# Down projection: ten steps of the second product ahead of the first product's last step

## The chip, the cores and the metric

The kernel runs on one core of one Trainium2 chip. The metric is device microseconds (us) of one execution. Engines are named as in the profile: PE is TensorE's matmul queue, PEld its weight loads, DVE is VectorE, ACT ScalarE, POOL GpSimd, SP SyncE. All DMAs of this kernel are issued from SP's queue, which the profile calls SPq.

## The reference, cut to what matters

A decoder trunk with two layers. Each layer ends with a gated feed-forward network. Its last product, `w_down`, is what the change touches; it runs once in each layer.

```python
D_MODEL, SEQ, DEPTH, D_FF = 1024, 1024, 2, 2816

def conv_ffn(h, w_up, conv_w, conv_b, w_down):
    u = h @ w_up
    ...
    a, b = u[..., :D_FF], u[..., D_FF:]
    return (jax.nn.silu(a) * b) @ w_down

for l in range(DEPTH):
    ...
    x = x + conv_ffn(rms_norm(x, ffn_norm[l]), w_up[l], conv_w[l], conv_b[l], w_down[l])
```

So the hidden activations are 1024 tokens by 2816 channels, and the down projection multiplies them by a 2816 x 1024 matrix.

## The kernel before

**Precision.** Each f32 operand is split into a high and a low part (`split`, L78): ACT writes the high part (L81), DVE subtracts it and writes the low part (L82). `mm3` (L153) issues three matmuls for each pair of tiles (L157 high by high, L158 high by low, L159 low by high).

**Seven products in place of eight.** `Up` (the up projection) and `Down` both use a Strassen-like scheme: the operands are cut into 2 x 2 blocks, and sums of blocks are multiplied seven times. For `Down` the left factors are the hidden activations. A hidden tile holds 128 channels by 1024 tokens, and there are 22. `Up.left` (L1355) takes tiles 2k and 2k+1 when both are done and makes seven factors of 128 x 512: four of them are halves of the tiles (one of these changed in place), and three are sums in buffers named `gs`. The sums are four POOL instructions (L1360 to L1363). `Up.store` (L1366) writes the seven factors to DRAM tile `gd_k`, with k from 0 to 10: two DMAs from the tiles (`gd<-v`), one from `gs`, two from the tiles, two from `gs`. The factors of the first and the second product are the first two written.

**Steps of Down.** A product i is a sum over k, so it has 11 steps (i, j), with j the index of the `gd` tile. In `Down.steps` (L1429) they stand product by product: (0, 0) to (0, 10), (1, 0) to (1, 10), and so on; `PRODUCTS` (L1419) says which factor and which block of `w_down` a product reads and where its sum goes. This text numbers steps by their place in the list: step 10 is the first product's last before the change. One step is 12 matmuls of 128 x 512: four row blocks times three. The first product sums into four PSUM banks named `psb` (`self.chain`), the second into four banks of two `psa` tiles. `add` (L1504) adds finished banks to x on DVE: after the second product both its own banks and the chain's; `psa` has two buffers, so the third product's first matmul waits for that add.

**Feeding a step.** `fetch` (L1448) reads the factors of two consecutive steps from `gd` into a `wr` tile (three buffers, L1457). `prep` (L1460) splits the factor and the block of `w_down` into `wh` and `wl` (four buffers each), three steps ahead of the step that is run, and calls `fetch` for pairs further on. The blocks of `w_down` are kept in SBUF (`hx` and `hT` tiles, `claim`, L1439), and `sums` (L1475) changes them in place on DVE for later products (L1478, L1480, L1482).

**What sets the order.** `Up.run` (L1372) is a table of slots: step 0 of Down is issued in slot 160, step 6 in slot 166, the last one; `left` and `store` of the last pair of hidden tiles stand in slots 164 and 166. After that `down_all` (L1116) issues the remaining steps. DVE's and ACT's order while `Up.run` is written is the order of the code; otherwise the framework's scheduler orders the instructions. SP's queue is in order: a DMA that waits for its data holds back every DMA behind it.

Of the kernel before, what the change touches and what calls it, by code (L numbers as in the profile page):

```python
# [22 lines left out]
CH = 512  # L23
# [19 lines left out]
class Trunk:  # L43
    def __init__(self, ctx, tc, a, out):
        self.tc, self.nc, self.a, self.out = tc, tc.nc, a, out
        e = ctx.enter_context
        self.cp = e(tc.tile_pool(name="cp", bufs=1))
        self.wp = e(tc.tile_pool(name="wp", bufs=1))
        self.hp = e(tc.tile_pool(name="hp", bufs=1))
        self.pp = e(tc.tile_pool(name="pp", bufs=1, space=PSUM))  # L50
        self.dp = e(tc.tile_pool(name="dp", bufs=1, space=DRAM))
        self.uid = 0
# [152 lines left out]
    def load_block(self, w, cols, gcol=None, step=2, pool=None):  # L205
        tiles = [self.load_rows(w, k0, min(step, KT - k0), cols, gcol, pool) for k0 in range(0, KT, step)]

        def at(kt, c0, n):
            hi, lo = tiles[kt // step]
            return hi[:, kt % step, c0:c0 + n], lo[:, kt % step, c0:c0 + n]  # L210
        return at
# [984 lines left out]
class Up:  # L1196
# [116 lines left out]
    def product(self, n, i):  # L1313

        s, add = self.st[n], self.k.nc.vector.tensor_tensor
        if i == 0:
            self.first(n)
        elif i == 1:
            self.second(n)
            self.take_second(n)  # L1320
        elif i == 2:
            self.third(n)
        elif i == 3:
            self.prod(n, s["c"], "s1", "t1", True)
            s["c5"] = self.copied(s["c"])
        elif i == 4:
            self.prod(n, s["p"], "s3", "t3", False)
            s["ub"] = self.k.sb(self.late, [P, S], F32, "u", 3)
            add(s["ub"][:, CH:], s["p"], s["c5"], ALU.add)
        elif i == 5:  # L1330
            self.prod(n, s["c"], "s4", "b22", False)
            add(s["ua"][:, CH:], s["c"], s["c2"], ALU.add)  # L1332
        else:
            self.prod(n, s["p"], "a22", "t4", False)
            self.k.nc.scalar.activation(s["ub"][:, :CH], s["p"], AF.Copy)
# [19 lines left out]
    def left(self, k):  # L1355

        g, h = self.hidden[2 * k:2 * k + 2]
        s1, s2, s4 = (self.k.sb(self.late, [P, CH], F32, "gs", 3) for _ in range(3))
        add = self.k.nc.gpsimd.tensor_tensor
        add(s1, g[:, CH:], h[:, CH:], ALU.add)  # L1360
        add(s2, s1, g[:, :CH], ALU.subtract)
        add(g[:, CH:], g[:, :CH], g[:, CH:], ALU.subtract)
        add(s4, h[:, :CH], s2, ALU.subtract)  # L1363
        self.factors = (g[:, :CH], h[:, :CH], s2, g[:, CH:], h[:, CH:], s1, s4)
# [49 lines left out]
class Down:  # L1414

    NK = NF // 2
# [5 lines left out]
    def __init__(self, k, l, gds, fx):  # L1422
        self.k, self.l, self.gds, self.fx = k, l, gds, fx
        self.w = k.a["w_down"][l]
        NK = self.NK
        self.names = {"x": [("b11", i) for i in range(NK)] + [("t3", i) for i in range(NK)] + [("b22", NK - 1)],
                      "h": [("b21", i) for i in range(NK)] + [(n, i) for i in range(NK) for n in ("b12", "b22")][:-1]}
        self.place = {}
        self.steps = [(i, j) for i in range(7) for j in range(NK)]  # L1429
        self.pairs = [(i, j, min(2, NK - j)) for i in range(7) for j in range(0, NK, 2)]  # L1430
        self.ready, self.raws, self.at_step = [], [], 0

    def claim_x(self):
# [26 lines left out]
    def prep(self, upto):  # L1460

        k = self.k
        while len(self.ready) < min(upto, len(self.steps)):
            i, j = self.steps[len(self.ready)]
            n = self.PRODUCTS[i][1]
            pair = i * (self.NK + 1) // 2 + j // 2
            self.fetch(pair + 1)
            hi, lo = k.whl([P, 2, CH])
            for x, src in enumerate((self.raws[pair][:, j % 2, :], self.place[n, j])):
                k.split(src, hi[:, x, :], lo[:, x, :])  # L1470
            self.ready.append((hi, lo))
            if j % 2 or j == self.NK - 1:
                self.fetch(pair + 4)
# [12 lines left out]
    def step(self):  # L1486
        k, n = self.k, self.at_step
        i, j = self.steps[n]
        _, _, run, dst = self.PRODUCTS[i]
        self.prep(n + 1 + self.AHEAD)  # L1490
        if n == 0:
            self.chain = [k.psb() for _ in range(4)]
        if j == 0:
            self.banks = self.chain if run else [t[:, x * CH:(x + 1) * CH] for t in (k.psa(), k.psa()) for x in range(2)]
        hi, lo = self.ready[n]
        first = i == 0 or not run
        for p in range(4):
            ps = slice(p * P, (p + 1) * P)
            k.mm3(self.banks[p], (hi[:, 0, ps], lo[:, 0, ps]), (hi[:, 1, :], lo[:, 1, :]), first and j == 0, j == self.NK - 1, not first)
        self.sums(i, j)  # L1500
        self.at_step += 1
        return i, j

    def add(self, i):  # L1504

        for banks in ((), (self.banks, self.chain))[i] if i < 2 else (self.banks,):
            for p in range(4):
                for rows, col in self.PRODUCTS[i][3]:
                    xs = self.k.x[:, rows * 4 + p, col * CH:(col + 1) * CH]
                    self.k.nc.vector.tensor_tensor(xs, banks[p], xs, ALU.add)  # L1510
# [57 lines left out]
```

## Time and profile before

| | |
|---|---|
| runs | 2602.53, 2613.72, 2611.74 us |
| median of the runs | 2611.74 us |
| profiled execution | span 2602.7 us; the profile gives no other time for it |
| PE busy | 2466.1 us (95%), 12306 matmuls |
| DVE busy | 1887.8 us (73%) |
| ACT busy | 1342.2 us (52%) |
| POOL busy | 751.8 us (29%) |
| chain that ended last | PE 71%, DVE 10%, ACT 6%, DMA 5%, POOL 4%, issue 3% |
| mean granted clock of PE | 0.988 of full speed |

The time line gives an instruction's start and length; "[10.22 <-ACT wh L81]" behind it means that its engine had stood idle for 10.22 us and what ended that. Buffer numbers are left out of names. Layer 0's down projection begins near 1156 us of the span, layer 1's near 2345 us.

### The profile page before, as it was taken

How to read it: one execution, taken by the hardware profiler on the slowest of the kernel's cores; microseconds unless marked ns; L12 is line 12 of the kernel's file. 1: busy time of each engine (PE TensorE's matmuls, PEld its weight loads, DVE VectorE, ACT ScalarE, POOL GpSimd, SP SyncE). 2: the span in 40 equal slices, each digit the busy share in tenths (PEclk: the TensorE clock that was granted, in tenths of full speed). 3: DMA queues.
4: the chain of work that ended last, by engine and by line, in shares of the span. 5: the costliest groups of instructions: out<-in, count | busy, mean ns of one | idle time of the engine just before them, and what ended most of it. 6: DMA issues, size and time to landing. Idle time of an engine off the chain costs nothing.

```text
span 2602.7 us, 35727 instructions
## 1 busy us (share of the span) xinstructions
PE 2466.1 (95%) x12306; PEld 2058.2 (79%) x12306; DVE 1887.8 (73%) x3207; ACT 1342.2 (52%) x2553; POOL 751.8 (29%) x616
## 2 busy tenths in 40 slices
PE   7898988988999999998999999999999999998998
PEld 7787777766778888886888988887777888886886
DVE  5757787888377878877665467878476778787765
ACT  5437777877145454443454356767244444443443
POOL 0105344444134554543000000000233455444000
PEclk9999999999999999999999999999999999999999
DMA  8473224333422333347334466666622233237523
GB/s 250 145 206 111 62 82 114 104 105 125 163 74 89 113 101 98 105 169 268 108 128 137 153 186 189 199 180 176 211 101 76 95 105 114 98 100 278 172 97 114
DMA packets 302701, 357.69 MB, mean 137 GB/s; under 512 B 37960, under 2 KB 183224, under 8 KB 302520
## 3 DMA queue, kind: packets, MB, share of 16 engines
q1 hardware_dynamic: 302520, 355.41, 42.9%
q8 instruction: 97, 1.59, 0.3%
q14 instruction: 84, 0.69, 0.1%
HBM read 245.55 MB, written 109.78 MB: 137 GB/s over the span
## 4 chain that ended last, share of the span: by engine, by line
PE 71%; DVE 10%; ACT 6%; DMA 5%; POOL 4%; issue 3%; SPq 0%; POOLq 0%; ACTq 0%; DVEq 0%
PE psa L157 12%; PE psa L158 12%; PE psa L159 12%; PE psb L157 9%; PE psb L159 9%; PE psb L158 8%; PE psa L300 3%; PE psb L399 3%; PE psb L422 3%; DVE pt L409 2%; ACT pt L406 1%; POOL gs L1360 1%; DVE ps L330 1%; POOL pw L366 1%; DVE wl L82 1%
## 5 line engine op out<-in xcount | busy, mean ns | idle before, releaser
L81 ACT ACTIVATE wh<-wr 128x512 fp32r<-128x512 f32 (+2 forms) x254 | 193.0, 763 | 357.6 <-PE psb L159 146.2
L82 DVE TENSOR_TENSOR wl<-wr,wh 128x512 fp32r<-128x512 f32 (+2 forms) x254 | 241.1, 953 | 166.8 <-ACT wh L81 166.1
L1345 DVE SCALAR_TENSOR_TENSOR v<-u,cw,v 128x1023 f32<-128x1023 f32 (+1 forms) x176 | 283.1, 1608 | 68.7 <-ACT v L1343 68.5
L409 DVE TENSOR_TENSOR pt<-psb,pt 128x512 fp32r<-128x512 f32 (+2 forms) x380 | 246.6, 658 | 62.1 <-ACT pt L406 59.0
L1343 ACT ACTIVATE v<-u,cw 128x1024 f32<-128x1024 f32 x88 | 109.6, 1246 | 309.9 <-DVE u L1332 283.2
L406 ACT ACTIVATE pt<-psb 128x512 fp32r<-128x512 f32 (+2 forms) x380 | 213.4, 571 | 88.7 <-PE psb L399 83.5
L422 PE MATMUL psb<-pt,vv 128*128 128x512 f32 (+2 forms) x864 | 225.8, 356 | 17.3 <-DVE pt L409 13.2
L157 PE MATMUL psa<-hT,wh 128*128 128x512 f32 x560 | 219.2, 392 | 5.3 <-DVE u L1306 5.3
L159 PE MATMUL psa<-hT,wl 128*128 128x512 f32 x560 | 218.7, 391 | 0.8 <-DVE wl L82 0.8
L158 PE MATMUL psa<-hT,wh 128*128 128x512 f32 x560 | 218.6, 390 | 0.0
L300 PE MATMUL psa<-kk,qq 128*128 128x512 f32 (+4 forms) x792 | 186.1, 350 | 20.1 <-DVE stat L330 12.3
L343 ACT ACTIVATE ps<-ps,stat 128x128 f32<-128x128 f32 (+1 forms) x192 | 147.8, 771 | 56.8 <-DVE stat L330 56.3
L422 PEld LDWEIGHTS psb<-pt,vv 128*128 128x128 f32 x864 | 141.4, 191 | 42.2 <-DVE pt L409 21.7
L121 POOL TENSOR_TENSOR rs<-ss,consts 128x1 f32<-128x1 f32 x44 | 25.8, 588 | 511.2 <-DVE ss L119 372.5
L481 POOL TENSOR_TENSOR wr<-wr 128x512 f32<-128x512 f32 x32 | 41.4, 1300 | 427.4 <-DMA kd<-st 244.5
L399 PE MATMUL psb<-consts,ps 128*128 128x128 f32 x928 | 149.2, 279 | 14.5 <-DVE pt L409 7.5
L157 PE MATMUL psb<-wh 128*128 128x512 f32 x352 | 139.8, 397 | 20.7 <-ACT wh L81 20.6
L157 PE MATMUL psb<-hT,wh 128*128 128x512 f32 x384 | 156.6, 408 | 1.0 <-DVE pt L409 0.9
L1247 POOL TENSOR_TENSOR ws<-wr 128x512 f32<-128x512 f32 x44 | 67.7, 1539 | 295.3 <-DMA wr<-in_w_up_dram 276.2
L159 PE MATMUL psb<-hT,wl 128*128 128x512 f32 x384 | 151.2, 394 | 0.0
L158 PE MATMUL psb<-hT,wh 128*128 128x512 f32 x384 | 150.8, 393 | 0.0
L300 PEld LDWEIGHTS psa<-kk,qq 128*128 128x128 f32 x792 | 121.6, 194 | 36.1 <-DVE stat L330 13.8
(287 smaller groups left out, 6831.0 us busy)
## 6 DMA issues: line engine op xcount, KB each, us to landing
wr<-in_w_up_dram SPq DMA_DIRECT2D x88, 512.0 KB
wr<-gd SPq DMA_DIRECT2D x154, 256.0 KB
gd<-v SPq DMA_DIRECT2D x88, 256.0 KB
gd<-gs SPq DMA_DIRECT2D x66, 256.0 KB
o<-ob SPq DMA_DIRECT2D x128, 128.0 KB
wr<-o SPq DMA_DIRECT2D x32, 512.0 KB
hT<-in_w_down_dram SPq DMA_DIRECT2D x64, 256.0 KB
qd<-st SPq DMA_DIRECT2D x56, 256.0 KB
```

The source lines that it names most:

```text
L81: nc.scalar.activation(hi, src, AF.Copy)
L82: nc.vector.tensor_tensor(lo, src, f32(hi), ALU.subtract)
L157: mm(out, lh, rh, start=first, stop=False, skip_group_check=more)
L158: mm(out, lh, rl, start=False, stop=False, skip_group_check=more)
L159: mm(out, ll, rh, start=False, stop=last, skip_group_check=more)
L300: nc.tensor.matmul(out, w, rhs, start=b not in banks[:i], stop=b not in banks[i + 1:])
L343: nc.scalar.activation(p, p, AF.Exp, bias=st[:, 0, ii:ii + 1], scale=-1.0, accum_out=st[:, 1, ii:ii + 1])
L399: nc.tensor.transpose(tp[0:kb, x:x + P], br["pt"][ii][:, o:o + kb], self.ident)
L406: nc.scalar.activation(st["hi"], st["src"], AF.Copy)
L409: self.nc.vector.tensor_tensor(st["lo"], st["src"], f32(st["hi"]), ALU.subtract)
L422: self.nc.tensor.matmul(out, v, t, start=st["begin"] and i == 0, stop=st["end"] and i == len(mms) - 1)
L1345: nc.vector.scalar_tensor_tensor(v[:, d:], u[:, :S - d], cw[:, tap, i:i + 1], v[:, d:], ALU.mult, ALU.add)
```

## The change

The list of steps of the first two products is written in another order: ten steps of the first product, ten of the second, then the last step of each. Steps 0 to 9 and 21 on are the same as before; step 10 is now (1, 0), step 19 is (1, 9), step 20 is (0, 10). The pairs for `fetch` follow the list, and a table says which pair a step belongs to. Since two products are now open at once, the banks are kept by product. No instruction is added or removed: 1494 DMAs, 12306 matmuls, 3209 DVE rows and 621 POOL rows stand in both.

```diff
-        self.steps = [(i, j) for i in range(7) for j in range(NK)]
-        self.pairs = [(i, j, min(2, NK - j)) for i in range(7) for j in range(0, NK, 2)]
+        self.steps = [(i, j) for i in range(2) for j in range(NK - 1)] + [(0, NK - 1), (1, NK - 1)]
+        self.steps += [(i, j) for i in range(2, 7) for j in range(NK)]
+        self.pairs = [(i, j, min(2, NK - j)) for i, j in self.steps if j % 2 == 0]
+        self.pair_of = {(i, j + x): k for k, (i, j, n) in enumerate(self.pairs) for x in range(n)}
+        self.banks = {}
...
-            pair = i * (self.NK + 1) // 2 + j // 2
+            pair = self.pair_of[i, j]
...
-            self.banks = self.chain if run else [t[:, x * CH:(x + 1) * CH] for t in (k.psa(), k.psa()) for x in range(2)]
+            self.banks[i] = self.chain if run else [t[:, x * CH:(x + 1) * CH] for t in (k.psa(), k.psa()) for x in range(2)]
...
-            k.mm3(self.banks[p], (hi[:, 0, ps], lo[:, 0, ps]), (hi[:, 1, :], lo[:, 1, :]), first and j == 0, j == self.NK - 1, not first)
+            k.mm3(self.banks[i][p], (hi[:, 0, ps], lo[:, 0, ps]), (hi[:, 1, :], lo[:, 1, :]), first and j == 0, j == self.NK - 1, not first)
...
-        for banks in ((), (self.banks, self.chain))[i] if i < 2 else (self.banks,):
+        for banks in ((), (self.banks[1], self.chain))[i] if i < 2 else (self.banks[i],):
```

On SP, layer 0, at the end of the up projection: `hT<-in_w_down` is the last claim of `w_down`, `gd_10` the last tile of factors, and `wr<-gd_0` to `wr<-gd_5` are fetches for the second product. Before:

```order
L1446 DMA hT_11258<-in_w_down_dram 128x512 x8
L1369 DMA gd_10_11386<-v_11102 128x512
L1369 DMA gd_10_11386<-v_11232 128x512
L1369 DMA gd_10_11386<-gs_11344 128x512
L1369 DMA gd_10_11386<-v_11102 128x512
L1369 DMA gd_10_11386<-v_11232 128x512
L1369 DMA gd_10_11386<-gs_11343 128x512
L1369 DMA gd_10_11386<-gs_11345 128x512
L1457 DMA wr_11400<-gd_10_11386 128x512
L1457 DMA wr_11402<-gd_0_8558 128x512
```

and with the change:

```order
L1460 DMA wr_11312<-gd_0_8558 128x512
L1460 DMA wr_11312<-gd_1_8841 128x512
L1460 DMA wr_11359<-gd_2_9124 128x512
L1460 DMA wr_11359<-gd_3_9407 128x512
L1369 DMA gd_10_11392<-v_11102 128x512
L1369 DMA gd_10_11392<-v_11232 128x512
L1369 DMA gd_10_11392<-gs_11347 128x512
L1369 DMA gd_10_11392<-v_11102 128x512
L1369 DMA gd_10_11392<-v_11232 128x512
L1369 DMA gd_10_11392<-gs_11346 128x512
L1369 DMA gd_10_11392<-gs_11348 128x512
L1460 DMA wr_11406<-gd_4_9690 128x512
```

The fetches for the second product's steps (1, 0) to (1, 3), now steps 10 to 13, have moved ahead of the stores of `gd_10`; the fetch for (1, 4), step 14, and all behind it still stand after the last store. The reads of `gd_10` (not shown) come later: six more fetches and two loads of x stand between the last store and the first of them.

On DVE, the same place: L82 are splits, L1478 and L1480 (L1481 and L1483 with the change) are in-place sums of blocks of `w_down`. Before, from step 10's first split to its second:

```order
L82 TENSOR_TENSOR wl_11437<-hx_11059,wh_11436 128x512
L1478 TENSOR_TENSOR hx_11230<-hT_11258 128x512 x3
L1478 TENSOR_TENSOR hx_11230<-hx_11230,hT_11258 128x512
L1480 TENSOR_TENSOR hx_11020<-hx_11059,hx_11020 128x512 x5
L1480 TENSOR_TENSOR hx_11020<-hx_11230,hx_11020 128x512 x3
L82 TENSOR_TENSOR wl_11437<-wr_11400,wh_11436 128x512
```

With the change step 10's first split is followed by the same three sums and then by step 10's second split; behind that, up to step 14's first split, stand:

```order
L82 TENSOR_TENSOR wl_11456<-hT_11119,wh_11455 128x512
L82 TENSOR_TENSOR wl_11456<-wr_11312,wh_11455 128x512
L1481 TENSOR_TENSOR hx_11230<-hx_11230,hT_11258 128x512
L1483 TENSOR_TENSOR hx_11020<-hx_11059,hx_11020 128x512
L82 TENSOR_TENSOR wl_11477<-wr_11359,wh_11476 128x512
L82 TENSOR_TENSOR wl_11477<-hT_11119,wh_11476 128x512
L1483 TENSOR_TENSOR hx_11020<-hx_11059,hx_11020 128x512 x3
L82 TENSOR_TENSOR wl_11495<-wr_11359,wh_11494 128x512
L82 TENSOR_TENSOR wl_11495<-hT_11119,wh_11494 128x512
L1483 TENSOR_TENSOR hx_11020<-hx_11059,hx_11020 128x512
L1483 TENSOR_TENSOR hx_11020<-hx_11230,hx_11020 128x512
L82 TENSOR_TENSOR wl_11519<-wr_11406,wh_11518 128x512
```

Between step 10's first split and the first split that waits for a fetch behind the stores, DVE has 12 instructions before and 17 with the change: two of the eight sums of L1480 have moved behind step 14's split, and seven splits of steps 10 to 13 have come in.

## Prediction

> **What bounds the kernel now.** PE is busy 95% of the span, and PE's own work does not change, so I looked for its idle time. First the page's costliest groups, then PE's time line around the first matmuls of step 10. Of PE's matmul groups on the page, this one has the most idle time ahead of it:
>
> ```profile
> L157 PE MATMUL psb<-wh 128*128 128x512 f32 x352 | 139.8, 397 | 20.7 <-ACT wh L81 20.6
> ```
>
> PE's time line puts all of it in two places (layer 0, layer 1):
>
> ```profile
> 1202.72 0.39 PE L159 MATMUL psb<-wh,wl 128*128 128x512 f32 x1
> 1213.33 0.79 PE L157 MATMUL psb<-wh 128*128 128x512 f32 x1 [10.22 <-ACT wh L81]
> ...
> 1218.32 0.39 PE L157 MATMUL psa<-wh 128*128 128x512 f32 x1
> ...
> 2393.84 0.39 PE L159 MATMUL psb<-wh,wl 128*128 128x512 f32 x1
> 2404.62 0.80 PE L157 MATMUL psb<-wh 128*128 128x512 f32 x1 [10.39 <-ACT wh L81]
> ...
> 2409.60 0.40 PE L157 MATMUL psa<-wh 128*128 128x512 f32 x1
> ```
>
> 1202.72 is the last matmul of step 9, 1213.33 the first of step 10, 1218.32 the first of step 11. The chain of waits says why, in layer 0 (layer 1's is the same to 0.1 us):
>
> ```profile
> 1187.60 17.23 POOL gs L1360
> 1204.91 1.26 POOL gs L1361
> 1206.17 1.23 POOL v L1362
> ...
> 1208.81 0.40 SPq L1369
> 1209.32 3.30 DMA wr<-gd
> 1212.64 0.64 ACT wh L81
> 1213.33 0.79 PE psb L157
> ```
>
> A POOL addition took 17.23 us that has a median of 1.29 (least, median and most, in ns, of the line's view):
>
> ```profile
> L1360 POOL TENSOR_TENSOR gs<-v,v x22: 1287/1287/17240, 812.7 to 2378.7; 128x512 f32<-128x512 f32 x22
> ```
>
> SP's queue shows what hung on it:
>
> ```profile
> 1183.07 6.27 SPq L1446 DMA_DIRECT2D hT<-in_w_down_dram  x8
> 1189.68 1.05 SPq L1369 DMA_DIRECT2D gd<-v  x2
> 1206.19 0.32 SPq L1369 DMA_DIRECT2D gd<-gs  x1
> ...
> 1209.32 2.65 SPq L1457 DMA_DIRECT2D wr<-gd  x5
> ```
>
> The factor that step 10 reads is the first stored, from `v` at 1189.68. Step 10 waited not for POOL's data but for its place in the queue: its fetch stands behind the `gs` stores, and those wait for POOL. And POOL waited for DVE:
>
> ```profile
> 1187.38 0.68 DVE L82 TENSOR_TENSOR wl<-wr,wh 128x512 fp32r<-128x512 f32 x1
> ...
> 1195.80 0.69 DVE L82 TENSOR_TENSOR wl<-hx,wh 128x512 fp32r<-128x512 f32 x1
> ...
> 1198.81 4.90 DVE L1480 TENSOR_TENSOR hx<-hx,hx 128x512 f32<-128x512 f32 x8
> 1213.31 0.69 DVE L82 TENSOR_TENSOR wl<-wr,wh 128x512 fp32r<-128x512 f32 x1 [9.60 <-ACT wh L81]
> ```
>
> ```profile
> 1187.50:1203.70 16.20, 15.61 (x69) 12.58 (x67) 16.20 (x27) 3.43 (x6) 16.11 (x1) 1.00 0.40 147
> 2378.70:2394.80 16.10, 15.53 (x69) 12.54 (x67) 16.10 (x27) 3.34 (x6) 16.09 (x1) 1.00 0.37 138
> ```
>
> The rows by stretch (length, then busy time and count of PE, PEld, DVE, ACT, POOL, then granted clock) show DVE busy without a gap (16.20 of 16.20, 27 instructions, so 0.60 each) while the one POOL instruction stands; DVE runs dry at 1198.81 + 4.90 = 1203.71, and POOL's next instruction starts 1.20 later. The same in both layers.
>
> **What the stall costs now.** From start to start 10.61 and 10.78 us, less the 0.23 of one matmul: 10.38 + 10.55. Then step 10 runs slowly, 1218.32 - 1213.33 = 4.99 and 4.98 in place of 2.72: 2.27 + 2.26. The 2.72 is the rhythm in which ACT gets a step's buffers back from PE:
>
> ```profile
> 1192.27 0.63 ACT L81 ACTIVATE wh<-wr 128x512 fp32r<-128x512 f32 x1 [1.56 <-PE psb L159]
> 1194.99 0.63 ACT L81 ACTIVATE wh<-hx 128x512 fp32r<-128x512 f32 x1 [1.57 <-PE psb L159]
> ...
> 1213.18 0.61 ACT L81 ACTIVATE wh<-hT 128x512 fp32r<-128x512 f32 x1
> ```
>
> Slow because of the granted clock, third from the right in the rows by stretch:
>
> ```profile
> 1196.00:1203.00 7.00, 7.00 (x32) 5.56 (x30) 7.00 (x12) 0.00 (x0) 7.00 (x1) 1.00 0.00 0
> 1203.00:1207.60 4.60, 0.11 (x1) 0.00 (x0) 0.71 (x2) 0.00 (x0) 4.52 (x4) 1.00 0.12 47
> 1207.70:1213.30 5.60, 0.00 (x0) 0.00 (x0) 0.00 (x0) 0.66 (x2) 0.91 (x1) 0.50 0.91 315
> 1213.40:1217.80 4.40, 4.40 (x11) 3.44 (x12) 4.16 (x7) 3.16 (x6) 0.00 (x0) 0.50 0.97 367
> ```
>
> Removable: 12.65 + 12.81 = **25.46 us**. The list of instructions is as long as before, so nothing else is saved or added but waits.
>
> **What the change puts in its place.** The reorder looks as if it gave ten steps, 27.2 us, of cover. It gives four: steps 10 to 13 are fetched ahead of the `gd_10` stores, but step 14's fetch stands behind them. So the same chain now ends at step 14.
>
> PE's side: step 9 ends at 1202.72 + 0.23 = 1202.95; four steps of 2.72 are 10.88, so PE wants step 14 at 1213.83. Its inputs are there: in-place blocks loaded before, and the 1 MB of fetches goes ahead of two stores of 0.5 MB, on DMA engines that carry nothing from 1196 to 1203 (the first of the four rows above, DMA share 0.00).
>
> The chain's side: up to 1195.80 DVE's order is the same, and from there it has 17 instructions in place of 12 before it must wait for step 14. It does not run dry between: step 12's first split stands 9 instructions on, 9 x 0.60 = 5.4 later, at 1201.2, and ACT has its high part at 1194.99 + 2 x 2.72 + 0.63 = 1201.06. That margin, 0.15 us, is the thinnest number here. So DVE stops 5 x 0.60 = 3.0 us later, at 1206.7, and everything hung on POOL comes 3.0 later: the fetch is issued at 1212.3, and ACT starts at 1212.64 + 3.0 = 1215.65. Step 10 had one operand split beforehand; step 14 has neither: ACT's second begins 0.54 later (1213.18 against 1212.64) and takes 0.61, and DVE's low part of it another 0.7, so the second matmul runs at 1217.6 in place of 1214.06: **3.5 us** lost. In layer 1 the same sum starts from this row,
>
> ```profile
> 2403.93 0.63 ACT L81 ACTIVATE wh<-wr 128x512 fp32r<-128x512 f32 x1 [17.20 <-DMA wr<-gd]
> ```
>
> so the second matmul runs at 2403.93 + 3.0 + 1.95 = 2408.9 in place of 2393.84 + 0.23 + 10.88 + 0.23 = 2405.2: 3.7. I take 3.6.
>
> Then no lead is left, and DVE has 3 sums and 2 splits a step, 5 x 0.60 = 3.0, against PE's 2.72: about 0.27 lost on steps 15 and 16 each, 0.54, until the sums thin out. Or the clock falls: idle of 10.2 us costs it, and what 3.0 to 3.6 us cost no row of a step shows. Near rows, PE idle of 2.6 and 2.8 us, and the clock behind each:
>
> ```profile
> 193.54 3.16 PE L300 MATMUL psa<-kk,qq 128*128 128x192 f32 x14 [2.59 <-DVE stat L330]
> 580.71 0.56 PE L300 MATMUL psa<-kk,qq 128*128 128x512 f32 x2 [2.84 <-DVE stat L355]
> ```
>
> ```profile
> 194.00:197.20 3.20, 3.20 (x15) 3.10 (x14) 1.74 (x5) 2.74 (x10) 1.29 (x1) 0.50 0.23 70
> 581.00:584.20 3.20, 2.96 (x18) 2.16 (x17) 3.20 (x12) 3.11 (x8) 3.20 (x4) 1.00 0.42 98
> ```
>
> One went to half speed for 3.2 us, one did not. Bounds: nothing, or half of 3.2, which is 1.6 (DVE catches up meanwhile, so 0.54 is in it). Between 0.54 and 1.6 I take 1.05, the middle, since the rows fall either way. The Trainium skill ("TensorE: Matmul & The Clock Gate", Part 1) says that the clock is judged in free-running windows of about 3.4 us and halved after an idle one; by it a wait of 3.6 halves it only where it covers a window, and a halved window costs 1.7. That agrees with one of the two rows going each way.
>
> Lost per layer: 3.6 + 1.05 = 4.65. **Sum: 25.46 - 2 x 4.65 = 16.2 us won** (15.1 with both clock drops, 17.2 with none).
>
> The two last steps, 20 and 21, I cost at nothing: the stores end some 20 us before, and six steps on PE cover their fetch. Their fetch waits for a `wr` buffer freed by step 15's splits, five DVE instructions behind step 14's, near 1217.5 + 3.0 = 1220.5, and takes 3.3; PE wants step 20 near 1214 + 4.65 + 6 x 2.72 = 1235. If that cover were gone it would show as PE idle before step 20. The wait after step 21, for DVE's add of the `psa` banks, keeps its place behind the same split and its 0.62 us:
>
> ```profile
> 1249.03 0.47 PE L157 MATMUL psa<-wh 128*128 128x512 f32 x1 [0.62 <-DVE x L1510]
> ```
>
> The second product's `psa` banks are wanted one step earlier; the up projection's results have been copied out of them before the last hidden tile is made, which is before L1360 can start at 1187.6.
>
> **Rivals.**
>
> *A, full cover.* POOL gets in before DVE runs dry. For it: where DVE had itself been held up, the two took turns:
>
> ```profile
> 818.87 2.30 POOL L1254 TENSOR_TENSOR ws<-wr,wr 128x512 f32<-128x512 f32 x1
> ...
> 819.92 2.33 DVE L82 TENSOR_TENSOR wl<-wr,wh 128x1024 fp32r<-128x1024 f32 x1
> ```
>
> and step 12's margin is 0.15 us: one gap there lets POOL in at 1201.2, and in turns of 1.2 and 0.6 it is through its four additions by 1208 (4 x 1.2 + 3 x 0.6 = 6.6), 3.7 us earlier than above. Step 14's loss is gone: 25.5 won. Against it: 27 instructions in a row left no gap, twice. The Trainium skill ("SBUF — State Buffer", Who interferes with whom) says that a DVE instruction with two SBUF inputs and a GpSimd one that reads SBUF hold the port for one instruction each, the first to issue ahead. Read so, POOL would wait for one DVE instruction, 0.7 us, and A would be certain; the trace's 17.23 speaks against that reading. Chance 0.2.
>
> *B, a second wait.* Steps 20 and 21 read `gd_10` behind loads of x, which stood behind the fetches for product two before. If these loads hold the queue for the memory of the closed pools, a wait comes back at step 20. My margin is some 9 us (1235 less 1.9 for the splits, against 1224); at 13 us late, 3 to 4 us more a layer are lost and some 9 won in all. Chance 0.15.
>
> *C, slower.* PE never gets the clock back: paced by DVE at 3.0 us a step it idles a little in every window, and steps 14 to 19 run at half speed. Price 6 x 2.72 = 16.3 + 3.6 = 19.9 a layer against 12.7 removed: 14 us slower. It decides once each window has enough idle. Against it: at half speed a step takes 5.4 us, DVE catches up at once, and PE is full again. Chance 0.05.
>
> **How the numbers follow.** Forecast 0.6, A 0.2, B 0.15, C 0.05. Against the profiled execution, whose span is 2602.7 (the fastest run took 2602.53, so nothing measurable lies around it), the sum gives 2586.5; against the runs' median, 2611.74, it gives 2595.5. The four known executions lie in two pairs 10 us apart, and I put the forecast at their mean: 2607.7 - 16.2 = **2591.5 us**. Range: A from the faster pair, 2602.6 - 25.5 = 2577, to the forecast's low end from the slower, 2613 - 15 = 2598, then on towards B, 2613 - 9 = 2604: 2602. Half a per cent, 13 us, is about what a measurement can tell from no change. Forecast and A are above it (0.8); the spread between runs moves 0.1 of that below: faster 0.7, same 0.25, slower 0.05.
>
> **What would show it.** Right: no idle of PE before the first `psa` matmul of step 10; a wait of about 3 us before step 14, released by ACT behind a fetch; L1360 on POOL near 20 us; its `gs` stores on SP 3 us later than before; no wait at step 20. A shows as L1360 under 15 us and no wait at step 14; B as idle before the `psb` matmuls of step 20; C as clock 0.50 for over 10 us. Wrong altogether if DVE's instructions behind 1195.80 are not back to back.

## The result and the profile after

| | before | with the change |
|---|---|---|
| median of the runs | 2611.26 us (4 runs: 2602.53 to 2613.72) | 2595.66 us (4 runs: 2593.97 to 2601.5) |
| ratio, 95% interval | | 0.9946 [0.9925, 0.9967] |
| span of the profiled execution | 2602.7 us | 2591.9 us (the execution took 2593.97) |
| PE busy | 2466.1 us | 2470.4 us |
| DVE, ACT, POOL busy | 1887.8, 1342.2, 751.8 us | 1878.4, 1342.0, 759.1 us |
| mean granted clock of PE | 0.988 | 0.988 |

The kernel is faster by 0.54%, and the interval leaves no change out. The medians are 15.6 us apart; by the interval the gain lies between 9 and 20 us.

The stall before step 10 is gone in both layers, and a shorter one stands before step 14. First the time line of the changed kernel, POOL, SP, ACT and DVE around layer 0's place (start, length, and in brackets the idle time before and what ended it):

```profile
1190.67 20.28 POOL L1360 TENSOR_TENSOR gs<-v,v 128x512 f32<-128x512 f32 x1 [25.15 <-DVE v L1352]
1211.03 1.29 POOL L1361 TENSOR_TENSOR gs<-gs,v 128x512 f32<-128x512 f32 x1
...
1192.65 2.31 SPq L1460 DMA_DIRECT2D wr<-gd  x4
1195.31 1.00 SPq L1369 DMA_DIRECT2D gd<-v  x2
1212.35 0.32 SPq L1369 DMA_DIRECT2D gd<-gs  x1
...
1215.47 3.15 SPq L1460 DMA_DIRECT2D wr<-gd  x6
...
1218.79 0.63 ACT L81 ACTIVATE wh<-wr 128x512 fp32r<-128x512 f32 x1 [11.41 <-DMA wr<-gd]
...
1219.45 0.69 DVE L82 TENSOR_TENSOR wl<-wr,wh 128x512 fp32r<-128x512 f32 x1 [9.65 <-ACT wh L81]
```

It is the chain of before, moved on by four steps: four fetches go out ahead of the stores (1192.65), the first `gs` store waits for POOL (1212.35), and step 14's fetch stands behind it (1215.47). L1360 now takes 20.28 us.

PE in the same time line, both layers: the last matmul of step 13, then the first and second of step 14.

```profile
1216.68 0.39 PE L159 MATMUL psa<-wh,wl 128*128 128x512 f32 x1
1220.00 0.50 PE L157 MATMUL psa<-wh 128*128 128x512 f32 x1 [2.93 <-ACT wh L81]
1220.81 0.80 PE L158 MATMUL psa<-wl,wh 128*128 128x512 f32 x1 [0.31 <-DVE wl L82]
...
2401.36 0.39 PE L159 MATMUL psa<-wh,wl 128*128 128x512 f32 x1
2404.88 0.65 PE L157 MATMUL psa<-wh 128*128 128x512 f32 x1 [3.13 <-ACT wh L81]
2405.69 0.79 PE L158 MATMUL psa<-wl,wh 128*128 128x512 f32 x1 [0.16 <-DVE wl L82]
```

In this trace matmuls at clock 1.00 start 0.23 apart. So the second matmul of step 14 is late by 1220.81 - 1216.68 - 2 x 0.23 = 3.67 us in layer 0, and by 3.87 in layer 1. No other idle time of PE over 0.5 us stands in the place but the old 0.62 before the third product; none before step 20.

The granted clock behind the two waits, from the rows by stretch (third number from the right):

```profile
1220.60:1223.70 3.10, 2.89 (x7) 2.31 (x8) 3.10 (x7) 2.57 (x5) 0.00 (x0) 0.51 1.05 403
1224.00:1230.00 6.00, 6.00 (x28) 4.93 (x27) 6.00 (x11) 2.31 (x4) 0.00 (x0) 0.99 0.95 353
...
2405.00:2408.20 3.20, 3.04 (x7) 2.09 (x8) 3.20 (x7) 2.67 (x6) 0.00 (x0) 0.51 1.00 355
```

PE ran at half speed for some 3 us in both layers, and then at full speed again.

**A ruler for the place.** The last gating instruction (L1352) comes before everything that differs, and the third product's first matmul, the one with the 0.62, comes behind it. From the start of the one to the start of the other is the length of the place. The rows of before (its layer 0 ends at 1249.03, a row that the prediction has):

```profile
1186.24 1.22 DVE L1352 TENSOR_TENSOR v<-v,v 128x1024 f32<-128x1024 f32 x1
...
2377.36 1.22 DVE L1352 TENSOR_TENSOR v<-v,v 128x1024 f32<-128x1024 f32 x1
...
2440.31 0.47 PE L157 MATMUL psa<-wh 128*128 128x512 f32 x1 [0.62 <-DVE x L1510]
```

and of the changed kernel:

```profile
1189.32 1.22 DVE L1352 TENSOR_TENSOR v<-v,v 128x1024 f32<-128x1024 f32 x1
...
1244.80 0.47 PE L157 MATMUL psa<-wh 128*128 128x512 f32 x1 [0.62 <-DVE x L1513]
...
2373.99 1.22 DVE L1352 TENSOR_TENSOR v<-v,v 128x1024 f32<-128x1024 f32 x1
...
2429.42 0.47 PE L157 MATMUL psa<-wh 128*128 128x512 f32 x1 [0.62 <-DVE x L1513]
```

Before: 62.79 and 62.95 us. With the change: 55.48 and 55.43. So 7.31 + 7.52 = 14.83 us are won in the place. The spans differ by 10.8 only: this execution was 1189.32 - 1186.24 = 3.08 late when it came to the first place, lost 0.86 more between the two, and 0.09 behind. That is spread between executions and not the change. Part of it can be read: at 712.33 PE had waited 2.45 us and ran on at a clock of 0.50 (in the execution of before, 2.10 us and 1.00), and by 771.48 this execution's lag had grown from 1.60 us to 3.07.

### The profile page after: what moved, and what is told of

It is laid out like the page before. It is cut to its first block, busy times and chain, and to the rows that moved or that the text cites. A ratio compares the mean times of both kernels' runs of the same rounds, so it can differ in the third digit from the quotient of the medians.

```text
span 2591.9 us, 35724 instructions
## 1 busy us (share of the span) xinstructions
PE 2470.4 (95%) x12306; PEld 2060.6 (79%) x12306; DVE 1878.4 (72%) x3207; ACT 1342.0 (52%) x2553; POOL 759.1 (29%) x616
## 4 chain that ended last, share of the span: by engine, by line
PE 71%; DVE 9%; ACT 6%; DMA 5%; POOL 4%; issue 3%; SPq 1%; POOLq 0%; ACTq 0%; DVEq 0%
PE psa L157 11%; PE psa L158 11%; PE psa L159 11%; PE psb L157 9%; PE psb L159 9%; PE psb L158 9%; PE psa L300 3%; PE psb L399 3%; PE psb L422 3%; DVE pt L409 2%; POOL gs L1360 2%; ACT pt L406 1%; DVE wl L82 1%; DVE ps L330 1%; POOL pw L366 1%
## 5 line engine op out<-in xcount | busy, mean ns | idle before, releaser
L82 DVE TENSOR_TENSOR wl<-wr,wh 128x512 fp32r<-128x512 f32 (+2 forms) x254 | 241.3, 954 | 152.7 <-ACT wh L81 152.0
L1345 DVE SCALAR_TENSOR_TENSOR v<-u,cw,v 128x1023 f32<-128x1023 f32 (+1 forms) x176 | 277.8, 1578 | 68.8 <-ACT v L1343 68.5
L399 PEld LDWEIGHTS psb<-consts,ps 128*128 128x128 f32 x928 | 113.4, 145 | 47.7 <-DVE pt L409 14.7
L330 DVE CUSTOM_DVE_ANT_0 ps<-psa,caub 128x128 f32<-128x128 f32 (+1 forms) x192 | 139.0, 751 | 14.0 <-PE psa L300 13.7
```

The costliest lines, as they stand in the source:

```text
L82: nc.vector.tensor_tensor(lo, src, f32(hi), ALU.subtract)
L330: self.nc.vector.tensor_tensor_reduce(p, s, br["spans"][ii][2], -1.0, 3e38, ALU.add, ALU.min, br["stat"][:, 0, ii:ii + 1])
L399: nc.tensor.transpose(tp[0:kb, x:x + P], br["pt"][ii][:, o:o + kb], self.ident)
L1345: nc.vector.scalar_tensor_tensor(v[:, d:], u[:, :S - d], cw[:, tap, i:i + 1], v[:, d:], ALU.mult, ALU.add)
```

## The experiments

Theory: PE waited because POOL, whose sums the `gs` stores need, is kept out as long as DVE runs instructions with two SBUF inputs back to back; the change only adds four steps of cover to that. Rivals: the move of steps is worth something by itself; only the place on SP's queue counts; POOL waits for DVE to be idle, whatever DVE runs. The place measured with the same ruler in every run:

| kernel | length of the place, layers 0 and 1 | median | ratio to before [95%] |
|---|---|---|---|
| before | 62.79, 62.95 | 2609.6 and 2612.86 (two sets of runs) | |
| changed | 55.48, 55.43 | 2595.66 | 0.9946 [0.9925, 0.9967] |
| 1: before, sums on DVE | 50.55, 50.56 | 2586.1 | 0.9902 [0.9888, 0.9916] |
| 2: changed, sums on DVE | 50.12, 50.12 | 2583.74 | 0.9905 [0.989, 0.992] |
| 3: changed, stores later | 56.73, 56.83 | 2597.71 | 0.9957 [0.9941, 0.9973] |
| 4: changed, one-input instruction | 50.14, 50.13 | 2582.88 | 0.9894 [0.9882, 0.9907] |
| 5: changed, a short one | 50.13, 50.14 | 2585.16 | 0.9895 [0.9882, 0.9908] |
| 6: changed, two-input instruction | 55.38, 55.93 | 2596.93 | 0.9944 [0.993, 0.9959] |
| 7: before, one-input instruction | 57.01, 55.87 | 2598.29 | 0.9945 [0.9931, 0.9959] |
| 8: before, stores on POOL's queue | 62.00, 62.13 | 2610.24 | 0.9993 [0.9984, 1.0001] |

Runs 1 to 4 go with the first set of before, 5 to 8 with the second, and the changed kernel with the 2611.26 above; across sets the gains are compared and not the medians. In run 3, layer 1, the wait at the end of the place is 1.15 us in place of 0.62. Where code is inserted, line numbers behind it differ by a few.

### 1. The kernel before, last pair's sums on DVE

```diff
-        add = self.k.nc.gpsimd.tensor_tensor
+        add = (self.k.nc.vector if k == NF // 2 - 1 else self.k.nc.gpsimd).tensor_tensor
```

> The kernel before, with the last pair's four sums on DVE in place of POOL; nothing is left out and no step is moved. My theory (the stall before step 10 is POOL kept out by DVE's back-to-back instructions, and its length is the 17.23 us of L1360 plus the three additions behind it): the four sums cost DVE about 4 x 0.6 = 2.4 us, the gs stores leave some 12 us earlier, PE shows no idle over 1 us before step 10, and the 25.5 us of the two stalls go: about 2586 us, 25 below the kernel before and 9 or 10 below the changed one. Rival (step 10 needs the lead that only the move of steps gives): PE still waits 5 us or more before step 10, and the time stays within 10 us of the kernel before.

The theory's main numbers came out: 2586.1 us, 23.5 below before, and no stall before step 10, though the steps stand in the old order. The first `gs` store left 4.36 us behind the start of L1352, where it had left 1206.19 - 1186.24 = 19.95 behind it: 15.6 us earlier and not some 12. PE's costliest wait of before (20.7 us ahead of these matmuls) in the same view of this kernel:

```profile
L157 PE MATMUL psb<-wh 128*128 128x512 f32 x352 | 137.5, 391 | 0.1
```

### 2. The changed kernel, last pair's sums on DVE

The same edit on the changed kernel.

> The changed kernel, with the last pair's four sums on DVE in place of POOL; nothing is left out. My theory: the wait before step 14 goes as well, so it gives about 2586 us, the same as the kernel before with this edit within 3 us; the move of steps is then worth nothing. Rival 1 (the move of steps brings something beside cover for this stall): over 5 us faster than the kernel before with this edit. Rival 2 (the wait before step 14 has another cause than POOL): a wait of 2 us or more stays before step 14 and the time stays near 2596.

The wait before step 14 is gone: of the idle time ahead of these matmuls only the two 0.62 are left.

```profile
L157 PE MATMUL psa<-wh 128*128 128x512 f32 x264 | 102.9, 390 | 1.2 <-DVE x L1513 1.2
```

Runs 1 and 2 are 2.4 us apart, their intervals almost the same, and their places 0.4 us a layer. With POOL out of the way the move of steps is worth next to nothing, so rival 1 of this run falls; and the wait before step 14 went with POOL, so its rival 2 falls too. Whether the place on SP's queue counts is left to runs 3 and 8.

### 3. The changed kernel, with two more steps of cover

```diff
     def store(self, k):
...
-        for j, t in enumerate(self.factors):
-            self.k.nc.sync.dma_start(gd[j], t)
+        self.later = [(gd[j], t) for j, t in enumerate(self.factors)]
         self.gds.append(gd)
+        self.send(2 if k == NF // 2 - 1 else 7)
+
+    def send(self, n):
+        for dst, t in self.later[:n]:
+            self.k.nc.sync.dma_start(dst, t)
+        self.later = self.later[n:]
...
             if slot >= 7 * NF + 6:
                 down.step()
+        self.send(5)
```

> The changed kernel, with five of the last pair's seven factor stores put behind the next fetch on SP's queue, so that steps 14 and 15 are fetched ahead of the stores that wait for POOL; nothing is left out. My theory (a race that more cover does not win: each step covered gives PE 2.72 us and DVE five more instructions, 3.0 us, to run without a gap): DVE runs 10 instructions longer, L1360 takes about 26 us in place of 20.28, the wait moves from step 14 to step 16, 3.5 to 4.5 us long in each layer, and the time is within 4 us of the changed kernel. Rival (only the place in the queue counts, two more steps are 5.4 us of cover): no wait over 1 us, and 10 us faster than the changed kernel.

The time line of POOL and PE, both layers:

```profile
1195.62 26.30 POOL L1360 TENSOR_TENSOR gs<-v,v 128x512 f32<-128x512 f32 x1 [25.19 <-DMA wr<-gd]
...
1231.17 0.80 PE L157 MATMUL psa<-wh 128*128 128x512 f32 x1 [3.70 <-ACT wh L81]
...
2383.62 26.30 POOL L1360 TENSOR_TENSOR gs<-v,v 128x512 f32<-128x512 f32 x1 [25.15 <-DMA wr<-gd]
...
2419.13 0.50 PE L157 MATMUL psa<-wh 128*128 128x512 f32 x1 [3.68 <-ACT wh L81]
```

L1360 grew by 26.30 - 20.28 = 6.02 us, the ten DVE instructions of 0.60 that two more steps bring. PE gained 2 x 2.72 = 5.44 of cover. The wait moved to step 16 and is 0.6 to 0.8 us longer. These two steps of cover do not win the race, since each step that covers the wait also feeds what makes it. So a better place on SP's queue is not enough by itself either.

### 4. and 5. The changed kernel, one DVE instruction with one input added

```diff
+    def probe(self):
+        out = self.k.sb(self.late, [P, 2], F32, "pr", 1)
+        self.k.nc.vector.reduce_max(out[:, 0:1], self.hidden[-1][:, :CH], axis=AX.X)
...
+        at(165, self.probe)
         for slot in range(7 * NF + 13):
```

Run 5 reads 16 elements a row (`:16`) in place of 512. Run 4:

> The changed kernel, with one added DVE instruction that reads one 128x512 input (a maximum along the row, whose result is used by nothing) behind step 7's splits, in the middle of the stretch in which POOL is kept out; nothing is left out. Theory 1 (it is DVE instructions with two SBUF inputs, back to back, that keep POOL out; one with a single input lets it in): L1360 ends beside the added instruction and takes under 10 us in place of 20.28; L1361 is then kept out in its turn for most of the rest, so the wait before step 14 gets shorter by at most 2 us. Theory 2 (POOL gets in only when DVE stands idle): L1360 stays at 20 to 21 us, and the time is that of the changed kernel plus at most 2 us.

Run 5:

> The changed kernel with the one-input DVE instruction cut from 512 elements a row to 16, so that it takes 0.1 to 0.2 us in place of 0.68; nothing else is left out. Theory 1 (the kind of the instruction decides, not its length): L1360 takes about 3.4 us as with the long one, and the time is within 3 us of that (2582.9). Theory 2 (POOL needs a while in which no second input is read, about as long as the instruction of 0.68): L1360 stays at 20 to 21 us and the time near the changed kernel's 2596.

One added instruction takes all of the stall away. POOL's time line in run 4, layer 0:

```profile
1190.92 3.43 POOL L1360 TENSOR_TENSOR gs<-v,v 128x512 f32<-128x512 f32 x1 [25.19 <-DVE v L1352]
1194.43 1.62 POOL L1361 TENSOR_TENSOR gs<-gs,v 128x512 f32<-128x512 f32 x1
1196.01 1.74 POOL L1362 TENSOR_TENSOR v<-v 128x512 f32<-128x512 f32 x1
1197.71 1.74 POOL L1363 TENSOR_TENSOR gs<-v,gs 128x512 f32<-128x512 f32 x1
```

and DVE's:

```profile
1193.12 0.68 DVE L1368 TENSOR_REDUCE pr<-v 128x1 f32<-128x512 f32 x1
1193.71 1.19 DVE L82 TENSOR_TENSOR wl<-wr,wh 128x512 fp32r<-128x512 f32 x1
1194.83 1.77 DVE L82 TENSOR_TENSOR wl<-hx,wh 128x512 fp32r<-128x512 f32 x1
1196.52 1.77 DVE L1486 TENSOR_TENSOR hx<-hT 128x512 f32<-128x512 f32 x1
1198.22 1.78 DVE L1486 TENSOR_TENSOR hx<-hT,hT 128x512 f32<-128x512 f32 x1
1199.92 0.68 DVE L1486 TENSOR_TENSOR hx<-hT 128x512 f32<-128x512 f32 x1
```

(`hx<-hT` is an sum whose two blocks both lie in `hT` tiles: it has two inputs as well.) L1360 ends 3.43 us after its start, beside the added instruction. The other half of theory 1 was wrong. I expected L1361 to be kept out in its turn, but from then on the two engines take turns: DVE's next four instructions take 1199.92 - 1193.71 = 6.21 us, not 2.4, and POOL is through all four sums by 1199.45. A wait that I thought would shrink by 2 us went altogether. "POOL gets in only when DVE stands idle" falls, as DVE never stands idle here. In run 5 the instruction is a quarter as long and does the same:

```profile
L1368 DVE TENSOR_REDUCE pr<-v x2: 159/162/164, 1197.4 to 2376.9; 128x1 f32<-128x16 f32 x2
```

(least, median and most, in ns). L1360 takes 3.43 us there too, so the kind of the instruction decides and not its length. Against the kernel before of their own set, runs 4 and 5 gain 26.7 and 27.7 us, run 2 25.9 and run 1 23.5, where the change gains 15.6; the intervals of these four overlap, so the medians do not separate them.

### 6. The changed kernel, a DVE instruction with two inputs added

The same place and length, but another kind:

```diff
+    def probe(self):
+        out = self.k.sb(self.late, [P, CH], F32, "pr", 1)
+        g = self.hidden[-1]
+        self.k.nc.vector.tensor_tensor(out, g[:, :CH], g[:, CH:], ALU.max)
```

> The changed kernel, with an added DVE instruction of the same length at the same place as the one-input one (behind step 7's splits), but reading two 128x512 inputs and writing 128x512, used by nothing; nothing is left out. Theory (it is the second SBUF input that keeps POOL out): L1360 takes 20.28 + 0.60, 20.9 us, PE waits about 3.6 us before step 14 in place of 2.9 to 3.1, and the time is that of the changed kernel plus 0 to 2 us, some 13 us above the one with one input. Rival (any added instruction there breaks the rhythm): L1360 under 10 us and no wait before step 14.

```profile
1193.55 20.28 POOL L1360 TENSOR_TENSOR gs<-v,v 128x512 f32<-128x512 f32 x1 [25.18 <-DVE v L1352]
...
1222.95 0.58 PE L157 MATMUL psa<-wh 128*128 128x512 f32 x1 [3.01 <-ACT wh L81]
```

Nothing is won: L1360 is that of the changed kernel, and PE's waits, 3.01 and 3.40 us, are near its 2.93 and 3.13 (about 3.6 was expected). L1360 did not grow by the expected 0.60, as one in-place sum fewer stands ahead of step 14's split in this kernel's order. So an added instruction does not by itself break the rhythm; the single input does. (The two kinds also differ in what they write, 128x512 here and 128x1 in runs 4 and 5. That was not varied alone.)

### 7. The kernel before, the one-input instruction added

The edit of run 4, with the steps in their old order.

> The kernel before, steps in their old order, with the one-input DVE instruction of the last run (a maximum along a 128x512 row, used by nothing) behind step 7's splits; nothing is left out. Theory (the only thing wrong was POOL being kept out, and one such instruction lets it in for good): L1360 takes 3 to 5 us in place of 17.23, POOL's four sums are through within 8 us, no idle of PE over 1 us before step 10, and the time is within 4 us of the changed kernel with the same instruction (2582.9). Rival (the move of steps is needed beside it): 5 us or more slower than that, with a wait left before step 10.

Here the theory fell and the rival came out: 2598.29 us, 13 above run 5 of the same set, with 3.92 and 3.93 us of wait. By the places it is 6.87 + 5.74 = 12.61 us above run 4. DVE and PE in the time line, layer 0:

```profile
1195.83 1.22 DVE L1352 TENSOR_TENSOR v<-v,v 128x1024 f32<-128x1024 f32 x1
...
1199.97 1.19 DVE L82 TENSOR_TENSOR wl<-wr,wh 128x512 fp32r<-128x512 f32 x1
...
1206.18 0.68 DVE L1483 TENSOR_TENSOR hx<-hT 128x512 f32<-128x512 f32 x1
...
1212.80 4.29 DVE L1485 TENSOR_TENSOR hx<-hx,hx 128x512 f32<-128x512 f32 x7
1217.02 0.68 DVE L82 TENSOR_TENSOR wl<-wr,wh 128x512 fp32r<-128x512 f32 x1
...
1217.76 1.22 PE L159 MATMUL psb<-wh,wl 128*128 128x512 f32 x2 [3.92 <-DVE wl L82]
```

POOL is early enough, and step 10's factor has arrived, for PE now waits for DVE's low part of it. DVE is not idle ahead of that split: it is late. In run 1, which has the same order of steps and no wait, the rows are

```profile
1192.90 1.22 DVE L1352 TENSOR_TENSOR v<-v,v 128x1024 f32<-128x1024 f32 x1
...
1207.88 2.49 DVE L1480 TENSOR_TENSOR hx<-hx,hx 128x512 f32<-128x512 f32 x4
1210.29 0.69 DVE L82 TENSOR_TENSOR wl<-wr,wh 128x512 fp32r<-128x512 f32 x1
```

From L1352 to the split are 17.39 us there and 21.19 here, 3.80 more. The turns with POOL cost 1206.18 - 1199.97 - 4 x 0.60 = 3.81, the added instruction 0.60, three more in-place sums ahead of the split (seven for four) 1.80; the four sums that DVE doesn't do here save 2.40. The sum is 3.81, against 3.80. So the move of steps is worth something after all, once POOL and DVE share: it gives DVE some slack ahead of its next urgent split, and the old order does not. The account closes, but no run took the turns' 3.8 us away alone.

### 8. The kernel before, five stores on POOL's own queue

```diff
-            self.k.nc.sync.dma_start(gd[j], t)
+            (self.k.nc.gpsimd if k == NF // 2 - 1 and j > 1 else self.k.nc.sync).dma_start(gd[j], t)
```

> The kernel before, steps in their old order, with the last pair's five later factor stores issued from POOL's own queue in place of SP's; POOL's sums stay on POOL and nothing is left out. Theory (PE waits for the place of step 10's fetch on SP's queue, not for POOL's data): L1360 stays kept out, 17 us or longer, since DVE has still less reason to stop, and yet PE has no idle over 1 us before step 10; the fetch is issued right behind the first two stores; about 2586 us. Rival (POOL being late matters by itself): PE waits 3 us or more before some step of the second or third product, and the time stays above 2595.

The first half came out: no wait before step 10, though L1360 takes 23.28 us. PE waited there for a place on SP's queue, not for POOL's data. The second half did not, and the time is that of before. SP, POOL and PE in the time line, layer 0:

```profile
1205.41 2.23 SPq L1457 DMA_DIRECT2D wr<-gd  x5
...
1225.59 1.07 POOL L1369 DMA_DIRECT2D gd<-gs  x2
...
1229.40 0.32 SPq L1123 DMA_DIRECT2D x<-xm  x1
1229.82 1.79 SPq L1457 DMA_DIRECT2D wr<-gd  x4
...
1234.74 0.80 PE L157 MATMUL psa<-wh 128*128 128x512 f32 x1 [8.87 <-ACT wh L81]
```

SP issues five fetches, and then a load of x holds the queue for over 20 us, until behind POOL's last store. Step 15's fetch stands behind it, and PE waits 8.87 us (9.08 in layer 1). That the load waits for memory which the late stores still hold is what the order of the rows suggests; it wasn't tried alone. The next transfer on SP that hangs on POOL took the place of the one removed.

## Why the prediction was right, point by point

**What is removable: right to a hundredth.** 12.65 + 12.81 = 25.46 us were forecast for the two stalls. The places with no wait left (run 4: 50.14 and 50.13) are shorter than those of before by 12.65 and 12.82; runs 2 and 5 give the same within 0.02 us.

**Four steps of cover, and the chain 3.0 us later: right.** L1360 was to take about 20 us and took 20.28. From L1352 to ACT's split of the awaited factor are 1218.79 - 1189.32 = 29.47 us, against 1212.64 - 1186.24 = 26.40 before: 3.07 later. The margin of 0.15 us at step 12's split held: ACT was through at 1203.50 + 0.63 = 1204.13, and DVE's split began at 1204.30.

**The new wait: right.** 3.6 us a layer were forecast; the second matmul of step 14 was 3.67 and 3.87 late.

**The clock: mis-sized.** The prediction bounded it by nothing (0.54 with DVE's catching up) and 1.6, and took the middle, 1.05. The places lost 62.79 - 50.14 = 12.65 less 7.31 won, 5.34, in layer 0, and 5.30 in layer 1. Less the wait that is 1.67 and 1.43 (the rows' 0.51 over 3.1 and 3.2 us makes 1.5 and 1.6): both layers paid about the upper bound. So 14.83 us were won in the place and not 16.2; the prediction's own figure for both clock drops was 15.1. The middle was no likely value. The prediction showed two waits of before, one each way, but the same view held six, of 2.59 to 2.88 us, and four of them (ending at 115.52, 193.54, 1452.24 and 1957.92) were followed, within 1.3 us, by some 3 us at a clock of 0.50. Two of the six, 2.64 and 2.63 us ahead of the same matmul in layers 0 and 1, parted:

```profile
768.60:771.80 3.20, 3.20 (x15) 2.63 (x15) 0.26 (x1) 0.00 (x0) 0.00 (x0) 1.00 0.00 0
1958.70:1961.90 3.20, 3.20 (x9) 2.50 (x8) 0.00 (x0) 0.00 (x0) 0.00 (x0) 0.50 0.02 5
```

So in these rows the clock fell to half or not at all, and the length of the wait alone did not decide. Behind the waits of 2.9 to 3.9 us in the place (two each in the changed kernel and in runs 3, 6 and 7) the granted clock, over some 3 us that begin at most 0.6 us after the wait's end, was between 0.50 and 0.66 all eight times. It was not certain to fall: elsewhere in run 4 a wait of 2.96 us, ending at 713.68, left it at 1.00. The Trainium skill ("TensorE: Matmul & The Clock Gate", Part 1) puts the window of the clock at about 3.4 us. A halved window is then worth some 1.7 us, an estimate from that figure, and 1.67 and 1.43 agree with it. That the clock is halved after an idle window, as the prediction quotes it, does not agree with waits of 2.59, 2.63 and 2.93 us that halved it, all shorter than such a window; the prediction was wrong to see its two rows as agreeing.

**The predicted time.** 2591.5 us was forecast and 2595.66 measured, within the range. Of the 4.2 us between, 3.6 lie in the base: the forecast was taken from 2607.7, the mean of four executions, and the kernel before has a median of 2611.26. One of the four was a span taken as a time, with nothing measurable around it; the changed kernel's execution of 2593.97 us had a span of 2591.9, so some 2 us do lie around it, 0.5 in the mean. The other 0.6 is the gain, 15.6 by the medians in place of 16.2. That these two are so close is partly luck: the medians cannot tell 15.6 from the 14.83 of the places.

**Rival A** (full cover, 25.5 us won) did not happen: while L1360 stood, 32 DVE instructions ran without letting POOL in, in both layers. Its price was right, as run 4 shows: 2609.6 - 2582.88 = 26.7 us. What was missing for it was not time but one DVE instruction of another kind. The Trainium skill ("SBUF — State Buffer", Who interferes with whom) says that two SBUF inputs of a DVE instruction contend with a GpSimd instruction that reads SBUF and that a `tensor_reduce` does not. Runs 4, 5 and 6 agree. Its lock that is held for one instruction at a time is what they show only after POOL had got in once; until then POOL lost to every instruction in a row, 26.30 us of them in run 3. **Rival B** (a wait before step 20) did not happen, though something like it can: in run 8 a load of x stood at the head of SP's queue for over 20 us, for a reason that was not tried alone. **Rival C** did not happen: the half speed ended after some 3 us in both layers.

## What to carry to other kernels

Look at what the transfer at the head of an in-order queue waits for, before reordering what waits behind it: here a reorder won 15 us, and one added DVE instruction of 0.16 us, on top of it, took away the rest of the stall. Where a POOL instruction takes many times its median while DVE is full of two-input instructions, move its work to DVE, or put one DVE instruction like that of run 5 (a maximum along the row: one input, one column out) behind the point where POOL becomes ready. Both engines then pay for sharing, so check that DVE's next urgent work has the slack.

## What was not expected of the hardware

- DVE and POOL have two ways of sharing. Under back-to-back two-input DVE instructions (0.60 us each) a POOL addition of 1.29 us stood 17.24, 20.28, 23.28 and 26.30 us, as long as DVE's stretch lasted. After a single one-input DVE instruction, even of 0.16 us, the two took turns: POOL's additions took 1.62 to 1.74 us and DVE's instructions came 1.70 apart.
- Waits of PE of 2.93 to 3.93 us were followed by a granted clock of 0.50 to 0.66 for some 3 us, all eight times in the place. Shorter ones go either way: 2.64 us left the clock at 1.00 in layer 0 of the kernel before, and 2.63 us halved it at the same matmul in layer 1.
